# A fixed opening: squares summed on the vector engine as x lands, silu(c) behind the root, modulation dots two to a tile

## The chip, the cores and the metric

The kernel runs on one core of one Trainium2 chip. The metric is device microseconds of one execution. The core has a matrix engine (PE; its weight loads are listed apart as PEld), a vector engine (DVE), a scalar engine (ACT), GpSimd (POOL), and SyncE (SP), which issues most transfers. Each engine works through its own queue in the order in which the program was written or scheduled, and semaphores hold an instruction back until what it needs is there.

## The reference, cut to what matters

Two layers, each a half-step SwiGLU FFN, a mixing block and another half-step FFN. x is 512 tokens by 1024 channels. Only the entry to the first FFN is touched by the change:

```python
c_act = jax.nn.silu(c)
mod = (c_act @ w_ada[l] + b_ada[l]).reshape(B, N_MOD, D_MODEL)   # shift, scale, gate, three times
hn = rms_norm(h, g_ffn1[l]) * (1.0 + sc1) + sh1
h = h + 0.5 * (1.0 + gt1) * swiglu(hn, w_ffn1_in[l], w_ffn1_out[l])
# rms_norm: y = xf * lax.rsqrt(jnp.mean(xf * xf, axis=-1, keepdims=True) + EPS);  y * gain
```

## The kernel before, in words

x is kept transposed, as eight tiles `h[0]` to `h[7]` of 128 channels by 512 tokens; four transfers bring two tiles each. A float32 product is done as three products of rounded parts: high by high, high by low, low by high (`wH`, `wL` of a weight tile; `hnH`, `hnL` of the normed input). ACT makes each high part by a cast, DVE the low part by a subtraction.

**The opening (`begin`)** computes the first norm and the first six output tiles of the first FFN. Nearly every instruction is pinned behind the one before it on its engine, so the order is as written. Three parts:

1. The head. PE runs products without a use (`warm`, 128x512), then turns c into a row repeated over all partitions (`ps_crep`, 8 products); ACT takes silu of it into `crep`. The squares of the eight tiles are made on DVE and ACT, and PE sums them over channels by 32 products of one column (`summed`, L1374, four per tile, into `ps_ss`). ACT takes the root (L1390), DVE the reciprocal (L1391), and four PE products (L1394) spread it over the partitions in `ps_rstd`.
2. The list `PLAN`, a string of tokens worked through in order by `step`. `z<k>` is h[k] times `ps_rstd` on DVE; `ada<k>`, `part<k>`, `col<k>`, `gm<k>` get scale and shift of tile k (k = 0, 1, 2) from PE; `d<k>`, `e<k>` get them (k = 3 to 7) by two dots of 1024 elements against `crep` on DVE (L1404); `x<k>` applies them on ACT, `H<k>` and `L<k>` make the two parts; `wH<n>`, `wL<n>` split weight tile n; `W<n>` is n warm products. `P<n><k><p>` is one of 144 PE products: output tile n, input tile k, part p. Each runs through the line L1419 (L1408 after the change).
3. Transfers: `fetch` brings a pair of modulation columns (1 MB, `wada`, four buffers), `fetch_w` a weight tile (0.5 MB, `wfirst`, four buffers). `more` says behind which token the later ones are issued.

**PSUM buffers.** PSUM tiles are taken from tags with two buffers each. A tile takes the buffer of the tile two earlier on its tag, and its first writer waits for the last reader of that one. The six output tiles take the tags by `("r0", "r1", "mm")[n % 3]`. So tag r1 goes to `ps_rstd`, then output tile 1, then output tile 4, which gets the buffer of `ps_rstd`; the last reader of that is the last `z` token in the order.

**Behind the opening (`ffn`)**, ten more output tiles of the first FFN follow, each of 24 products (L127 to L129), with weights streamed through two `wraw` buffers; then products in pairs (`pair_in`, L431 to L433) begin. Between them, `ada_steps` puts dots of the next modulation vector (L197, 8 here, each against its own 0.5 MB transfer issued by POOL), spread over the tile pairs j by a tuple.

Of the kernel before, what the change touches and what calls it, by code (L numbers as in the profile page):

```python
# [17 lines left out]
P = 128  # L18
# [3 lines left out]
KD = D // P  # L22
# [4 lines left out]
NB = T // P  # L27
# [3 lines left out]
BASE = 16  # L31
PAD = 24
PLAN = """
z0 ada0 z1 z7 part0 wH0 W1 col0 z6 gm0 z2 W4 ada1 z4 x0 z3 H0 wL0 part1 P00a wH1 col1 L0 P00c P10a gm1 P00b P10b wL1 x1 ada2 H1 z5 P10c part2 P01a L1
P01c wH2 col2 P01b gm2 P11a wL2 P20a x2 P20b P11c P11b P21a H2 P21b d3 P20c P21c P02a wH3 P02c P12a P12c L2 P22a P22c P30a e3 P30b P31a P31b P02b P12b
P22b P32a wL3 P32b x3 H3 d4 W3 P30c P31c P32c P03a P03c P13a L3 P13c P23a P23c e4 wH4 P03b P13b P23b P33a P33c P33b P40a d5 P40b x4 P41a P41b P42a
P42b H4 P43a d6 P43b P04a P04c P14a wH5 P14c L4 P24a P24c P34a e6 P34c P50a P50b P51a P51b P52a P52b P53a wL5 x6 P53b P04b P14b P24b H6 P34b d7 P44a
P50c P51c P52c P53c P44b L6 P54a P54b P54c e5 P06a P06c P06b P16a P16c P16b P26a P26c e7 x5 P26b P36a P36c P36b H5 P46a P46b P56a wL4 x7 P05a P05c
P15a P15c H7 P25a L5 P25c P40c P41c P42c L7 P43c P44c P05b P15b P25b P35a P35c P35b P45a P45c P45b P55a P55c P55b P46c P56c P56b P07a P07c P07b P17a
P17c P17b P27a P27c P27b P37a P37c P37b P47a P47c P47b P57a P57c P57b  # L40
""".split()
GROUPS = ((0, 12), (12, 22))
STEP = 0.65
# [25 lines left out]
def trunk_kernel(ctx, tc, ins, out, layers=L, phases=("ffn1", "mix", "ffn2")):  # L69
# [12 lines left out]
    act, mm = nc.scalar.activation, nc.tensor.matmul  # L82

    def E(name="e", dt=F32):
        return sp.tile([P, T], dt, name=name, tag="e", bufs=4)
# [4 lines left out]
    def psum(shape, name, tag="x"):  # L90
        return ps.tile(shape, F32, name=name, tag=tag, bufs=2)
# [60 lines left out]
    h = []  # L152
# [84 lines left out]
    def new_ss():  # L237
        return sp.tile([P, T], F32, name="ss", tag="ss")
# [111 lines left out]
    def ffn(l, w_in, w_pair, w_out, hn, im, ss, need, then, first, ready, coming):  # L350
# [6 lines left out]
        with tc.tile_pool(name="act", bufs=1) as ap_:  # L357
# [153 lines left out]
            for g, (j0, j1) in enumerate(GROUPS):  # L511
                for p in range(j0 // 2, j1 // 2):
                    if p < n_first:
                        X = new_x(p)
                        for j in (2 * p, 2 * p + 1):
                            pg = next(tiles)
                            beside(2 * j)
                            pu = next(tiles)
                            s = E("silu")
                            act(pg.like(s), pg.view, AF.Silu)  # L520
                            for seen, part in pu.pieces(s):
                                stt(part, part, -1.0, seen, ALU.mult, ALU.mult)
                            nc.scalar.copy(xs[j][0], s)
                            behind = tt(xs[j][1], s, xs[j][0].bitcast(F32), ALU.subtract)
                            beside(2 * j + 1)
                            if n_first == 4:
                                ada_steps(ap_, crep, (4, 4, 0, 0, 0, 0, 0, 0)[j], behind)
                    else:
                        after[0] = None if g or p > n_first + 1 else loads[-2]
                        pair_in(p)  # L530
                        after[0] = None
                flush()
                if g and ss is not None:

                    act(E("none")[:, :1], xs[j1 - 1][0][:, :1].bitcast(F32), AF.Sqrt, bias=vals["eps"], scale=0.0)
                if todo and not crep:
                    with tc.issue_after(loads[-1].ins):
                        crep = ada_crep(ap_)
                if g == 0:
                    cg = small_.tile([P, KD], F32, name="cg", tag="cg")  # L540
                    if n_first == 4:
                        ada_until(ap_, crep, l, im + 2)
                k1 = 0
                for i in range(KD - 2 * g):
                    if i < 7 - g:
                        many = 3 * (i < 6) if not g else (2, 3, 3, 3, 3, 2)[i] if n_first == 4 else (3, 3, 3, 2, 2, 2)[i]
# [770 lines left out]
    def begin(pool):  # L1317
# [6 lines left out]
        def pin(e, m):  # L1324

            if e in behind:
                tc.add_manual_dep(m.ins, behind[e].ins.name, ORDER, reason="the opening keeps its order")
            behind[e] = m
            return m
# [3 lines left out]
        def fetch():  # L1333
            w = pool.tile([P, 2 * D], F32, name="wada", tag="wada", bufs=4)
            nc.sync.dma_start(w, ins["wa0"][len(wa)])
            wa.append(w)

        def fetch_w():
            j, g = divmod(len(wf), 2)
            w = pool.tile([P, KD, P], F32, name="wfirst", tag="wfirst", bufs=4)  # L1340
            nc.sync.dma_start(w, ins["w1i"][0, j, g])
            wf.append(w)

# [3 lines left out]
        def warm(n):  # L1347

            for _ in range(n):
                pin("PE", mm(pw.rearrange("p (a b) -> p a b", b=P), ones_r, wide, start=True, stop=True))  # L1350
# [3 lines left out]
        nc.gpsimd.tensor_copy(cz[:, :, 0], cact)  # L1354
        warm(3)
        crep = pool.tile([P, D], F32, name="crep", tag="crep")
        for hf in range(2):
            pt = psum([P, 4, P], "ps_crep")
            for k in range(4):
                pin("PE", mm(pt[:, k], cT[:, 4 * hf + k : 4 * hf + k + 1].to_broadcast([P, P]), cst("ident"), start=True, stop=True))  # L1360
            pin("ACT", act(crep[:, hf * 512 : hf * 512 + 512], pt.rearrange("p k n -> p (k n)"), AF.Silu))
            if hf == 0:
                sqs = [E("sq") for _ in range(2)]
                for i in range(2):
                    pin("ACT", act(sqs[i], h[i], AF.Square))
        pin("ACT", act(col["sh0"][:, :1], cact[:, :1], AF.Sqrt, bias=vals["eps"], scale=0.0))
        for _ in range(4):
            fetch()
            fetch_w()
        pt = psum([P, NB], "ps_ss")  # L1370

        def summed(i):
            for b in range(NB):
                m = mm(pt[:, b : b + 1], sqs[i][:, b * P : (b + 1) * P], ones[:, :1], start=i + b == 0, stop=i == KD - 1, skip_group_check=True)  # L1374
                pin("PE", m)

        summed(0)
        summed(1)
        for i in range(2, KD):
            sqs.append(E("sq"))  # L1380
            if i in (5, 7):
                pin("ACT", act(sqs[i], h[i], AF.Square))
            else:
                pin("DVE", tt(sqs[i], h[i], h[i], ALU.mult))
            if i % 2 == 0:
                warm(4)
            summed(i)
        warm(3)
        r = pool.tile([P, NB], F32, name="rstd_t", tag="rstd_t")
        pin("ACT", act(r, pt, AF.Sqrt, bias=vals["eps"], scale=1.0 / D))  # L1390
        pin("DVE", nc.vector.reciprocal(r, r))  # L1391
        rstd = psum([P, T], "ps_rstd", "r1")
        for b in range(NB):
            pin("PE", mm(rstd[:, b * P : (b + 1) * P], r[:, b : b + 1].to_broadcast([P, P]), cst("ident"), start=True, stop=True))  # L1394
        pin("DVE", stt(col["gb"], bsc, 1.0, g1, ALU.add, ALU.mult))
        zs, ws, part, sums, pts = {}, {}, {}, {}, {}

# [5 lines left out]
            w = wa[k][:, half : half + D]  # L1403
            pin("DVE", stt(w, w, 1.0, crep, ALU.mult, ALU.mult, accum_out=col[name][:, k : k + 1]))  # L1404

        more = {"ada0": (fetch,), "ada1": (fetch, fetch_w), "ada2": (fetch,), "wL1": (fetch_w,), "e3": (fetch,)}

        def step(token):  # L1408
            kind = "P" if token[0] == "P" else token.rstrip("0123456789")
# [10 lines left out]
                return  # L1420
            k = int(k)
            c = slice(k, k + 1)
            if kind == "z":
                zs[k] = pool.tile([P, T], F32, name="z", tag="z", bufs=KD)
                pin("DVE", tt(zs[k], h[k], rstd, ALU.mult))
# [156 lines left out]
```

## Time and profile before

| | |
|---|---|
| three runs | 1813.88, 1818.63, 1819.55 us; median 1818.63 us |
| the profiled execution | 1815.97 us, span 1814.2 us, granted clock 0.993 |
| busy share of the span | PE 98%, PEld 90%, DVE 74%, ACT 46%, POOL 8% |
| first P product | starts 31.08 us into the span |
| last P product of the opening | starts 65.68 us |
| first product of the pairs (L431) | starts 121.37 us |

A row of a timeline gives start, length, engine, line, operation, output and inputs, how many rows were merged, and in brackets how long the engine stood idle before it and what ended that. Matmul rows overlap each other, so successive starts, not lengths, give the pace of PE.

### The profile page before, as it was taken

The numbers are of one execution on the slowest core, as the hardware profiler recorded it, in microseconds if no ns is written. First come the engines' busy times: TensorE is split into PE (matmuls) and PEld (weight loads), VectorE is DVE, ScalarE is ACT, GpSimd is POOL, SyncE is SP. The second block draws the span as 40 slices with busy tenths as digits, with TensorE's granted clock in tenths as the row PEclk, the third lists the DMA queues.
The fourth block names the chain that finished last, engine by engine and source line by source line (L and its number), as shares of the span: only waits on it lengthen the run. The fifth ranks groups of instructions, "written<-read, shape, count | busy, mean of one in ns | idle before, by whom it ended". The sixth has DMA issues, their size and how long they took to land.

```text
span 1814.2 us, 33785 instructions
## 1 busy us (share of the span) xinstructions
PE 1785.9 (98%) x13898; PEld 1629.1 (90%) x13898; DVE 1347.8 (74%) x2181; ACT 840.0 (46%) x1292; POOL 142.8 (8%) x227
## 2 busy tenths in 40 slices
PE   9999999999999999999999999999999999999999
PEld 7789899898768999899999989999877798999998
DVE  4688677877777878678878786778686788864862
ACT  4444255374433555255445524544654445533551
POOL 0101100101000000100100010110000000010000
PEclk8999999999999999999999999999999999999999
DMA  8567877713123476976738687673421427685742
GB/s 313 190 194 208 271 198 204 249 53 102 57 83 119 140 201 177 303 192 192 239 107 214 177 284 205 187 230 130 122 64 41 141 79 196 186 235 137 200 140 70
DMA packets 91404, 309.93 MB, mean 171 GB/s; under 512 B 10416, under 2 KB 11184, under 8 KB 90224
## 3 DMA queue, kind: packets, MB, share of 16 engines
q1 hardware_dynamic: 61920, 201.58, 33.1%
q0 software_dynamic: 29328, 106.18, 23.5%
q8 instruction: 109, 1.79, 0.4%
q14 instruction: 47, 0.39, 0.1%
HBM read 303.79 MB, written 3.93 MB: 170 GB/s over the span
## 4 chain that ended last, share of the span: by engine, by line
PE 80%; DVE 9%; DMA 4%; ACT 4%; issue 2%; POOL 0%; ACTq 0%; DVEq 0%; SPq 0%; POOLq 0%
PE ps_mm L127 12%; PE ps_mm L128 12%; PE ps_mm L129 12%; PE ps_d L431 7%; PE ps_d L432 7%; PE ps_d L433 7%; PE ps_f L432 3%; PE ps_f L433 3%; PE ps_f L431 3%; DVE wL L141 2%; PE ps_g L432 2%; PE ps_g L433 2%; PE ps_g L431 2%; PE ps_mm L1419 2%; DMA wada<-in_wadaT 2%
## 5 line engine op out<-in xcount | busy, mean ns | idle before, releaser
L139 ACT CAST wH<-wraw 128x1024 fp32r<-128x1024 f32 (+2 forms) x290 | 264.0, 916 | 472.6 <-PE ps_mm L128 215.1
L141 DVE TENSOR_TENSOR wL<-wraw,wH 128x1024 fp32r<-128x1024 f32 (+2 forms) x290 | 306.0, 1059 | 120.1 <-ACT wH L139 118.3
L127 PE MATMUL ps_mm<-actH,wH 128*128 128x512 f32 (+1 forms) x784 | 281.0, 358 | 0.0
L128 PE MATMUL ps_mm<-actL,wH 128*128 128x512 f32 (+1 forms) x784 | 280.5, 358 | 0.0
L129 PE MATMUL ps_mm<-actH,wL 128*128 128x512 f32 (+1 forms) x784 | 280.5, 358 | 0.0
L129 PE MATMUL ps_mm<-hnH,wL 128*128 128x512 f32 (+1 forms) x712 | 245.0, 346 | 3.6 <-DVE wL L141 3.6
L127 PE MATMUL ps_mm<-hnH,wH 128*128 128x512 f32 (+1 forms) x712 | 247.3, 354 | 1.3 <-ACT hnH L289 0.9
L128 PE MATMUL ps_mm<-hnL,wH 128*128 128x512 f32 (+1 forms) x712 | 246.2, 348 | 0.1
L431 PE MATMUL ps_d<-comH,wH 128*128 128x256 f32 x816 | 225.2, 276 | 1.2 <-ACT s L457 1.2
L432 PE MATMUL ps_d<-comL,wH 128*128 128x256 f32 x816 | 224.4, 275 | 0.0
L433 PE MATMUL ps_d<-comH,wL 128*128 128x256 f32 x816 | 224.4, 275 | 0.0
L141 DVE TENSOR_TENSOR wL<-sum,wH 128x1024 fp32r<-128x1024 f32 x102 | 125.0, 1226 | 83.4 <-ACT wH L139 83.3
L197 DVE SCALAR_TENSOR_TENSOR wada<-wada,crep 128x1024 f32<-128x1024 f32 x128 | 153.5, 1221 | 37.5 <-DMA wada<-in_wadaT 37.3
L129 PEld LDWEIGHTS ps_mm<-actH,wL 128*128 128x128 f32 x784 | 148.7, 190 | 16.8
L128 PEld LDWEIGHTS ps_mm<-actL,wH 128*128 128x128 f32 x784 | 148.7, 190 | 16.7
L127 PEld LDWEIGHTS ps_mm<-actH,wH 128*128 128x128 f32 x784 | 148.7, 190 | 16.6
L431 PEld LDWEIGHTS ps_d<-comH,wH 128*128 128x128 f32 x816 | 156.6, 192 | 2.8 <-ACT s L457 2.8
L433 PEld LDWEIGHTS ps_d<-comH,wL 128*128 128x128 f32 x816 | 156.7, 192 | 0.0
L432 PEld LDWEIGHTS ps_d<-comL,wH 128*128 128x128 f32 x816 | 156.6, 192 | 0.0
L139 ACT CAST wH<-sum 128x1024 fp32r<-128x1024 f32 x102 | 106.8, 1047 | 105.0 <-PE ps_f L432 42.4
L127 PEld LDWEIGHTS ps_mm<-hnH,wH 128*128 128x128 f32 x712 | 133.5, 191 | 21.5 <-issue 7.6
L129 PEld LDWEIGHTS ps_mm<-hnH,wL 128*128 128x128 f32 x712 | 135.6, 190 | 17.8 <-DVE wL L141 4.8
(384 smaller groups left out, 3884.1 us busy)
## 6 DMA issues: line engine op xcount, KB each, us to landing
wada<-in_wadaT POOLq DMA_DIRECT2D x128, 512.0 KB, 4.8
wraw<-in_wmi SPq DMA_DIRECT2D x40, 512.0 KB, 3.6
wraw<-in_w2p SPq DMA_DIRECT2D x36, 512.0 KB, 4.2
wraw<-in_w1p SPq DMA_DIRECT2D x32, 512.0 KB, 5.0
wraw<-in_w1o SPq DMA_DIRECT2D x32, 384.0 KB, 4.5
wraw<-in_w2o SPq DMA_DIRECT2D x32, 384.0 KB, 4.5
wraw<-in_w1o SPq DMA_DIRECT2D x32, 320.0 KB, 4.0
wraw<-in_w2o SPq DMA_DIRECT2D x32, 320.0 KB, 3.5
```

What stands on the lines that cost most here:

```text
L127: mm(acc, wH, xH, start=start, stop=False)
L128: mm(acc, wH, xL, start=False, stop=False)
L129: latest["large"] = mm(acc, wL, xH, start=False, stop=stop)
L139: nc.scalar.copy(hi, src)
L141: return nc.vector.tensor_sub(lo, src, hi.bitcast(F32))
L197: stt(w, w, 1.0, crep, ALU.mult, ALU.mult, accum_out=out_)
L431: mm(acc, wH, xH, start=start and i + k == 0, stop=False, skip_group_check=True)
L432: mm(acc, wH, xL, start=False, stop=False, skip_group_check=True)
L433: mm(acc, wL, xH, start=False, stop=k == 3, skip_group_check=True)
L1419: latest["large"] = pin("PE", mm(paired(pts[n]), w, x, start=first, stop=last, skip_group_check=True))
```

## The change

Squares: ACT writes the square of h[0] straight into a sum tile `ss`, squares the others but h[3], and DVE adds them up as they come. The square of h[7] is not added: PE sums it and `ss` over channels by four one-column products each, 8 instead of 32. The root's activation table is loaded ahead of the squares, silu(c) moves behind the root (tokens `s0`, `s1`), the spreading of the reciprocal becomes a token (`R0`) behind `ada0`, fourteen warm products stand ahead of the 8 products, `wfirst` gets a fifth buffer, `PLAN` and `more` are new, and the eight dots in `ffn` are spread over four tile pairs.

```diff
-z0 ada0 z1 z7 part0 wH0 W1 col0 z6 gm0 z2 W4 ada1 z4 x0 z3 H0 wL0 part1 P00a wH1 col1 L0 P00c P10a gm1 P00b P10b wL1 x1 ada2 H1 z5 P10c part2 P01a L1
+ada0 R0 W1 s0 part0 wH0 col0 z0 gm0 s1 z4 W1 ada1 x0 z3 H0 z2 part1 P00a L0 wH1 col1 z1 P00b wH2 P10a wL1 P10b W1 P20a P20b gm1 P10c wL2 x1 ada2 H1
...
-                                ada_steps(ap_, crep, (4, 4, 0, 0, 0, 0, 0, 0)[j], behind)
+                                ada_steps(ap_, crep, (0, 2, 2, 2, 2, 0, 0, 0)[j], behind)
...
-            w = pool.tile([P, KD, P], F32, name="wfirst", tag="wfirst", bufs=4)
+            w = pool.tile([P, KD, P], F32, name="wfirst", tag="wfirst", bufs=5)
...
-        for hf in range(2):
-            pt = psum([P, 4, P], "ps_crep")
-            for k in range(4):
-                pin("PE", mm(pt[:, k], cT[:, 4 * hf + k : 4 * hf + k + 1].to_broadcast([P, P]), cst("ident"), start=True, stop=True))
-            pin("ACT", act(crep[:, hf * 512 : hf * 512 + 512], pt.rearrange("p k n -> p (k n)"), AF.Silu))
-            if hf == 0:
-                sqs = [E("sq") for _ in range(2)]
-                for i in range(2):
-                    pin("ACT", act(sqs[i], h[i], AF.Square))
         pin("ACT", act(col["sh0"][:, :1], cact[:, :1], AF.Sqrt, bias=vals["eps"], scale=0.0))
-        for _ in range(4):
-            fetch()
-            fetch_w()
+        turned = [psum([P, 4, P], "ps_crep", "r0") for _ in range(2)]
+        for k in range(KD):
+            pin("PE", mm(turned[k // 4][:, k % 4], cT[:, k : k + 1].to_broadcast([P, P]), cst("ident"), start=True, stop=True))
+        warm(14)
+        ss, sqs = new_ss(), {}
+        for i in range(KD):
+            if i:
+                sqs[i] = E("sq")
+            if i == 3:
+                pin("DVE", tt(sqs[3], h[3], h[3], ALU.mult))
+            else:
+                pin("ACT", act(sqs[i] if i else ss, h[i], AF.Square))
+            if i in (3, 4, 5, 6):
+                for j in range(1, 4) if i == 3 else (i,):
+                    pin("DVE", tt(ss, ss, sqs[j], ALU.add))
+        for f in (fetch, fetch_w, fetch, fetch_w, fetch_w, fetch, fetch_w, fetch):
+            f()
         pt = psum([P, NB], "ps_ss")
-        summed(0)
...
+        for n, x in enumerate((sqs[7], ss)):
             for b in range(NB):
+                pin("PE", mm(pt[:, b : b + 1], x[:, b * P : (b + 1) * P], ones[:, :1], start=n + b == 0, stop=n == 1, skip_group_check=True))
+        warm(2)
...
-        more = {"ada0": (fetch,), "ada1": (fetch, fetch_w), "ada2": (fetch,), "wL1": (fetch_w,), "e3": (fetch,)}
+        more = {"ada0": (fetch, fetch_w), "ada1": (fetch,), "wL0": (fetch_w, fetch), "e3": (fetch,)}
...
+            if kind == "R":
+                for b in range(NB):
+                    pin("PE", mm(rstd[:, b * P : (b + 1) * P], r[:, b : b + 1].to_broadcast([P, P]), cst("ident"), start=True, stop=True))
+            elif kind == "s":
+                pin("ACT", act(crep[:, k * 512 : k * 512 + 512], turned[k].rearrange("p k n -> p (k n)"), AF.Silu))
```

**Place 1: PE, the head.** `sq_149` to `sq_227` are the squares of h[0] to h[7], `wada_160` the first modulation columns. Before, from the second group of squares on:

```order
L1350 MATMUL ps_warm_135<-ones_r_100 128x512 x4
L1374 MATMUL ps_ss_176<-ones_r_100,sq_185 128x1 x4
L1374 MATMUL ps_ss_176<-ones_r_100,sq_195 128x1 x4
L1350 MATMUL ps_warm_135<-ones_r_100 128x512 x4
L1374 MATMUL ps_ss_176<-ones_r_100,sq_201 128x1 x4
L1374 MATMUL ps_ss_176<-ones_r_100,sq_211 128x1 x4
L1350 MATMUL ps_warm_135<-ones_r_100 128x512 x4
L1374 MATMUL ps_ss_176<-ones_r_100,sq_217 128x1 x4
L1374 MATMUL ps_ss_176<-ones_r_100,sq_227 128x1 x4
L1350 MATMUL ps_warm_135<-ones_r_100 128x512 x3
L1394 MATMUL ps_rstd_239<-con_83,rstd_t_236 128x128 x4
L1442 MATMUL ps_ada_247<-wada_160,cz_136 32x256 x8
```

After, `sq_188` is the square of h[7] and `ss_168` the sum of the other seven:

```order
L1360 MATMUL ps_crep_145<-con_83,cT_81 128x128 x4
L1350 MATMUL ps_warm_135<-ones_r_100 128x512 x14
L1378 MATMUL ps_ss_206<-ones_r_100,sq_188 128x1 x4
L1378 MATMUL ps_ss_206<-ones_r_100,ss_168 128x1 x4
L1350 MATMUL ps_warm_135<-ones_r_100 128x512 x2
L1436 MATMUL ps_ada_222<-wada_190,cz_136 32x256 x8
L1414 MATMUL ps_rstd_220<-con_83,rstd_t_217 128x128 x4
```

The one-column products are down to two groups of four, the warm products stand in one block, and the spreading has moved behind `ada0`.

**Place 2: PE, the first product of output tile 4 (`P40a`).** Before, as its row 91 (`ps_mm_420`), 48 P products come ahead of it:

```order
L1419 MATMUL ps_mm_376<-hnL_121,wH_367 128x512
L1419 MATMUL ps_mm_420<-hnH_114,wH_411 128x512 [waits Activation_49]
L1419 MATMUL ps_mm_420<-hnL_115,wH_411 128x512
L1419 MATMUL ps_mm_420<-hnH_116,wH_411 128x512
L1419 MATMUL ps_mm_420<-hnL_117,wH_411 128x512
```

After (`ps_mm_375`), 36 P products come ahead of it:

```order
L1408 MATMUL ps_mm_335<-hnH_118,wH_324 128x512
L1408 MATMUL ps_mm_335<-hnH_118,wL_325 128x512
L1408 MATMUL ps_mm_335<-hnL_119,wH_324 128x512
L1408 MATMUL ps_mm_375<-hnH_114,wH_367 128x512 [waits DVE_49,Activation_49]
L1408 MATMUL ps_mm_375<-hnL_115,wH_367 128x512
```

Output tile 4 comes 12 products earlier, and its first product now has a wait on DVE besides the one on ACT for its weights.

**Place 3: DVE, the last reader of `ps_rstd`.** Before, the last `z` (`z_335`, token `z5`) stands between the low parts of the second weight tile and of the second input tile:

```order
L1437 TENSOR_TENSOR wL_306<-wfirst_166,wH_305 128x1024 [waits DMAHW2_49,Activation_49]
L1425 TENSOR_TENSOR z_335<-h4_89,ps_rstd_239 128x512
L1431 TENSOR_TENSOR hnL_117<-z_258,hnH_116 128x512 [waits Activation_49]
L1399 SCALAR_TENSOR_TENSOR gm0_133<-ps_col_346,par_93,gb_130 128x1 [waits PE_49]
L1400 TENSOR_TENSOR sh0_134<-ps_col_346,par_93 128x1
```

After, it (`z_468`) stands behind all six weight splits, six low parts and eight of the ten dots; `wada_360` is the last modulation pair to be fetched:

```order
L1393 SCALAR_TENSOR_TENSOR wada_360,sc_131<-wada_360,crep_142 128x1024 [waits DMAHW4_49]
L1419 TENSOR_TENSOR z_449<-h6_91,ps_rstd_220 128x512
L1431 TENSOR_TENSOR hnL_127<-z_394,hnH_126 128x512 [waits Activation_49]
L1393 SCALAR_TENSOR_TENSOR wada_360,sh_132<-wada_360,crep_142 128x1024
L1388 SCALAR_TENSOR_TENSOR gm0_133<-sc_131,par_93,gb_130 128x1 [waits DVE_49]
L1389 TENSOR_TENSOR sh0_134<-sh_132,par_93 128x1 [waits DVE_49]
L1419 TENSOR_TENSOR z_468<-h4_89,ps_rstd_220 128x512
```

The `z` tokens were all early before; now `z6`, `z7` and `z5` come late, `z5` stands in PLAN behind 63 P tokens of which `P40a` is the first.

**Place 4: DVE, the dots behind the opening.** Before, `wL_649` is the split of the third weight tile there:

```order
L524 TENSOR_TENSOR actL_610<-silu_611,actH_609 128x512 [waits Activation_49]
L197 SCALAR_TENSOR_TENSOR wada_579,mod0_2_585<-wada_579,crep_562 128x1024 [waits DMASW2_49]
L197 SCALAR_TENSOR_TENSOR wada_581,mod0_2_585<-wada_581,crep_562 128x1024 [waits DMASW3_49]
L141 TENSOR_TENSOR wL_649<-wraw_647,wH_648 128x1024 [waits DMAHW0_49,Activation_49]
L197 SCALAR_TENSOR_TENSOR wada_583,mod0_2_585<-wada_583,crep_562 128x1024 [waits DMASW4_49,DVE_49]
```

After, that split is `wL_615`:

```order
L524 TENSOR_TENSOR actL_569<-silu_570,actH_568 128x512 [waits Activation_49]
L141 TENSOR_TENSOR wL_584<-wraw_582,wH_583 128x1024 [waits DMAHW7_49]
L141 TENSOR_TENSOR wL_615<-wraw_613,wH_614 128x1024 [waits DMAHW0_49,Activation_49]
L197 SCALAR_TENSOR_TENSOR wada_560,mod0_2_564<-wada_560,crep_540 128x1024 [waits DMAHW1_49,DMASW1_49]
L197 SCALAR_TENSOR_TENSOR wada_562,mod0_2_564<-wada_562,crep_540 128x1024 [waits DMASW2_49]
```

Three dots stood ahead of the third split; now none does.

More of the change, by code (lines that the diff above doesn't have):

```diff
@@ L33 @@
 PLAN = """
-z0 ada0 z1 z7 part0 wH0 W1 col0 z6 gm0 z2 W4 ada1 z4 x0 z3 H0 wL0 part1 P00a wH1 col1 L0 P00c P10a gm1 P00b P10b wL1 x1 ada2 H1 z5 P10c part2 P01a L1
[L35 to L40, printed above, removed]
+ada0 R0 W1 s0 part0 wH0 col0 z0 gm0 s1 z4 W1 ada1 x0 z3 H0 z2 part1 P00a L0 wH1 col1 z1 P00b wH2 P10a wL1 P10b W1 P20a P20b gm1 P10c wL2 x1 ada2 H1
+wL0 P20c part2 P01a P11a wH3 col2 L1 P00c P01c gm2 P30a P30b wL3 x2 P01b P11c P11b P21a H2 P21c d3 P21b P30c P31a P31b P31c P02a L2 P02c P12a P12c e3
+P22a P02b P12b P22c P22b wH4 P32a P32c P32b d4 x3 P40a P40b P41a P41b wL4 H3 P42a P42b P03a P03c P13a L3 P40c P41c wH5 P42c z6 P03b P13c P13b e4 P23a
+P23c P50a P50b P51a P51b P52a wL5 P52b x4 P23b P33a P33c P33b H4 P43a d6 P50c P51c P52c P43c P43b P53a L4 P53b P53c P04a e6 P04c P04b P14a P14c P14b
+P24a P24c d7 x6 P24b P34a P34c P34b H6 P44a P44c z7 P44b P54a P54c L6 P54b P06a P06c e7 P06b P16a P16c P16b P26a P26c P26b z5 P36a x7 P36c P36b P46a
+d5 P46c H7 P46b P56a P56c P56b L7 P07a P07c P17a e5 P17c P07b P17b P27a P27c P27b P37a P37c x5 P37b P47a P47c P47b H5 P57a P57c P57b L5 P05a P05c P15a
+P15c P05b P15b P25a P25c P25b P35a P35c P35b P45a P45c P45b P55a P55c P55b
 """.split()
@@ L1370, in begin @@
         pt = psum([P, NB], "ps_ss")
-        def summed(i):
+        for n, x in enumerate((sqs[7], ss)):
             for b in range(NB):
-                m = mm(pt[:, b : b + 1], sqs[i][:, b * P : (b + 1) * P], ones[:, :1], start=i + b == 0, stop=i == KD - 1, skip_group_check=True)
-                pin("PE", m)
-        summed(0)
[L1378 to L1387, printed above, removed]
@@ L1388, in begin @@
-        warm(3)
+                pin("PE", mm(pt[:, b : b + 1], x[:, b * P : (b + 1) * P], ones[:, :1], start=n + b == 0, stop=n == 1, skip_group_check=True))
+        warm(2)
         r = pool.tile([P, NB], F32, name="rstd_t", tag="rstd_t")
@@ L1392, in begin @@
         rstd = psum([P, T], "ps_rstd", "r1")
-        for b in range(NB):
-            pin("PE", mm(rstd[:, b * P : (b + 1) * P], r[:, b : b + 1].to_broadcast([P, P]), cst("ident"), start=True, stop=True))
         pin("DVE", stt(col["gb"], bsc, 1.0, g1, ALU.add, ALU.mult))
```

## The prediction

> **What bounds the kernel now.** First the page: PE is busy nearly throughout and its clock is full but for the first of 40 slices.
>
> ```profile
> PE 1785.9 (98%) x13898; PEld 1629.1 (90%) x13898; DVE 1347.8 (74%) x2181; ACT 840.0 (46%) x1292; POOL 142.8 (8%) x227
> PEclk8999999999999999999999999999999999999999
> ```
>
> So time can only be won where PE works on something else than products, or slowly: in the opening. Then the timeline of PE there, with where the products of the opening start and end and where the pairs begin, and below it windows (start and end, length, busy time of PE, PEld, DVE, ACT, POOL, granted clock, share of the DMA engines, GB/s).
>
> ```profile
> 2.38 1.65 PE L1350 MATMUL ps_warm<-ones_r 128*128 128x512 f32 x3 [2.38 <-ACT ones_r L165]
> 7.24 2.05 PE L1374 MATMUL ps_ss<-ones_r,sq 128*128 128x1 f32 x16
> 19.55 3.41 PE L1374 MATMUL ps_ss<-ones_r,sq 128*128 128x1 f32 x16
> 24.24 1.91 PE L1394 MATMUL ps_rstd<-con,rstd_t 128*128 128x128 f32 x8
> 30.08 1.07 PE L1442 MATMUL ps_ada<-wada,cz 128*32 128x256 f32 x16
> 31.08 0.48 PE L1419 MATMUL ps_mm<-hnH,wH 128*128 128x512 f32 x1
> 65.68 0.38 PE L1419 MATMUL ps_mm<-hnL,wH 128*128 128x512 f32 x1
> 65.89 0.46 PE L127 MATMUL ps_mm<-hnH,wH 128*128 128x512 f32 x1
> 121.37 0.27 PE L431 MATMUL ps_f<-comH,wH 128*128 128x256 f32 x1
> ```
>
> ```profile
> 7.66:11.07 3.41, 3.41 (x27) 3.24 (x28) 1.55 (x3) 2.52 (x4) 0.00 (x0) 1.00 1.04 427
> 11.07:14.48 3.41, 3.41 (x14) 3.02 (x14) 0.69 (x1) 0.63 (x1) 0.00 (x0) 0.50 1.03 423
> 24.72:28.13 3.41, 3.41 (x24) 1.92 (x23) 1.94 (x4) 0.05 (x1) 0.00 (x0) 0.50 0.02 8
> 28.13:31.00 2.87, 2.87 (x25) 1.61 (x25) 2.39 (x6) 2.71 (x4) 0.00 (x0) 1.00 0.52 174
> ```
>
> PE is never without a row in the head, yet from 7.24 to 26 these are one-column products, warm products and the spreading, which lead to the root and no further; from 11.07 to 28.13 they run at half clock (the same sixteen rows take 3.41 in place of 2.05). Transfers fill that time at over 400 GB/s and then stop (8 GB/s), since no buffer is free. From 31.08 PE runs products at 65.89 - 65.68 = 0.21 us each (0.2155 by longer stretches of such rows).
>
> **The change: the head.** Eight groups of one-column products become two, while squares and adds hide under the landing of x.
>
> ```profile
> 1.65 1.85 SPq L155 DMA_DIRECT2D h<-in_xT  x4
> DMA to landing us min/median/max: 4.3/5.5/6.7
> 7.22 2.08 DVE L1384 TENSOR_TENSOR sq<-h 128x512 f32<-128x512 f32 x3 [6.19 <-DMA h<-in_xT]
> 8.10 1.28 ACT L1366 ACT_TABLE_LOAD   x1
> 22.99 0.26 ACT L1390 ACTIVATE rstd_t<-ps_ss,v_eps 128x4 f32<-128x4 f32 x1 [9.61 <-PE ps_ss L1374]
> 23.29 0.18 DVE L1391 RECIPROCAL rstd_t<-rstd_t 128x4 f32<-128x4 f32 x1 [11.46 <-ACT rstd_t L1390]
> 26.19 2.48 DVE L1425 TENSOR_TENSOR z<-h,ps_rstd 128x512 f32<-128x512 f32 x4 [2.67 <-PE ps_rstd L1394]
> 28.35 1.05 ACT L1435 CAST wH<-wfirst 128x1024 fp32r<-128x1024 f32 x1
> 29.47 0.82 ACT L1427 ACTIVATE z<-z,sh,gm 128x512 f32<-128x512 f32 x1
> 30.32 0.62 ACT L1429 CAST hnH<-z 128x512 fp32r<-128x512 f32 x1
> ```
>
> The last pair of x lands at 3.1 + 6.7 = 9.8. Two squares on ACT end near 11.0, the sixth add on DVE (7.22 + 7 x 0.69) near 12.1; the fourteen warm products, of 512 columns like the P products (0.2155 each), fill PE from 7.4 to 10.5, when the square they stand ahead of is not ready either, so they cost nothing; at the pace of the first three (1.65 / 3 = 0.55) they would run to 15 and cost 4. Four products on the sum take 2.05 / 4 = 0.5 to 1.0: the sum stands by 13.1, root and reciprocal (22.99 to 23.47) add 0.5. On PE two warm products and `ada0` (0.5 + 1.07) come first: 14.7; the spreading takes 0.96 to 1.91. So z0 starts at 15.8, at half clock 17.3, against 26.19. Silu(c), moved behind the root, brings a table load and two activations in front of `x0` on ACT: from the root at 13.5 the load 1.28, the two silus and the copy for `part0` at some 0.6 each (as the cast of 512 columns at 30.32), the cast of the first weight tile 1.05, x0 0.82 and H0 0.6 add up to 5.6 and end at 19. Its cover is z0, `gm0` and three more z on DVE until 18.7; what shows of the move is about 0.5, and 1 to 2 if the load comes late. The first P product comes near 19 in place of 31.08.
>
> On SP the first eight loads keep their bytes; the third weight tile goes ahead of the third modulation pair, and the fifth `wfirst` buffer lets the fifth weight tile go out without waiting for a split. POOL's one store of `crep` stays behind DVE's last work of the opening. I cost these at nothing by themselves: what counts is when the last modulation pair lands, below.
>
> **The change: output tile 4.** That gain meets a wait. `ps_rstd`, output tile 1 and output tile 4 share the two buffers of tag r1, so `P40a` waits for the last reader of `ps_rstd`, `z5`. Before, it is read early:
>
> ```profile
> 34.21 0.68 DVE L1425 TENSOR_TENSOR z<-h,ps_rstd 128x512 f32<-128x512 f32 x1
> ```
>
> At 34.2 nothing waits for it; now `z5` is the 42nd instruction of DVE from z0 on, behind dots that wait for transfers. PE gets 36 of the 144 products done and stops; the 108 others are queued behind it, though ACT has the parts of more input tiles ready, and everything of the FFN waits for PE. When z5 is read comes out of DVE's sum, by successive starts:
>
> ```profile
> 44.40 0.22 DVE L1399 SCALAR_TENSOR_TENSOR gm<-sc,par,gb 128x1 f32<-128x1 f32 x1
> 44.60 1.22 DVE L1404 SCALAR_TENSOR_TENSOR wada<-wada,crep 128x1024 f32<-128x1024 f32 x1
> 45.75 1.22 DVE L1404 SCALAR_TENSOR_TENSOR wada<-wada,crep 128x1024 f32<-128x1024 f32 x1
> 46.89 0.69 DVE L1431 TENSOR_TENSOR hnL<-z,hnH 128x512 fp32r<-128x512 f32 x1
> 48.84 1.22 DVE L1437 TENSOR_TENSOR wL<-wfirst,wH 128x1024 fp32r<-128x1024 f32 x1
> 49.98 1.22 DVE L1404 SCALAR_TENSOR_TENSOR wada<-wada,crep 128x1024 f32<-128x1024 f32 x1
> ```
>
> Eight dots and six weight splits at 1.14, eight z and six low parts at 0.61, seven pairs of gm and sh at 0.20: 16.0 + 8.5 + 1.4 = 25.9. From 15.8 to 17.3 that gives 41.7 to 43.2 with no wait in it. Transfers bound it too:
>
> ```profile
> wada<-in_wa SPq DMA_DIRECT2D x8, 1024.0 KB, 7.5
> wfirst<-in_w1i SPq DMA_DIRECT2D x6, 512.0 KB, 10.4
> 21.31:24.72 3.41, 3.41 (x14) 3.12 (x15) 0.23 (x2) 0.26 (x1) 0.00 (x0) 0.50 0.79 321
> ```
>
> The first loads, up to the fourth pair and the fourth weight tile, end near 24 as now (321 GB/s in the last row, 423 when full); four more of 1.05 MB and two of 0.52 MB at 423 GB/s end at 36.5, or 38.5 if some 2 us are lost between them; d7, z7, L6, e7, gm and z5 behind the last add 4.3: 41 to 43. With some waits for weights on both, I take z5 read at 44.0 (42.4 to 46).
>
> PE has its 36 done near 29 to 30: the last part that they need, L2, is DVE's 11.2 us of work after z0 (15.8 + 11.2 = 27, and a little for waits), with eight products behind it. So the stop is some 14 us long. PE's longest wait in the trace of before, once it has begun, is 2.3:
>
> ```profile
> PE ps_t L659 <- DVE X L996: 4.6, 2, 2.3
> ```
>
> So what 14 us do to the clock isn't seen, and is bounded: nothing (a gain is excluded, full clock being the most that the rows show), or half clock as in the 17.1 us from 11.07 to 28.13 (a loss of 8.5). Nearest is the start of the program: PE runs from 2.38, and the products are at their fast pace only from about 7.4, 5 us at half pace, a loss of 2.5. I take 2.5.
>
> [...]
>
> Then 108 products: 44.1 + 108 x 0.2155 + 2.5 = 69.9 for the first L127, against 65.89: 4.0 later. Bounds: 42.5 + 23.3 = 65.8 with no loss of clock (0.1 earlier) and 46.1 + 23.3 + 2.5 = 71.9 (6.0 later); the 8.5 is rival B.
>
> **The change: dots behind the opening.** From 65.89 to 121.37 PE does 240 products, 51.7 us, so 3.8 are lost:
>
> ```profile
> PE ps_mm L129 <- DVE wL L141: 3.1, 2, 1.8
> 76.30 1.23 DVE L197 SCALAR_TENSOR_TENSOR wada<-wada,crep 128x1024 f32<-128x1024 f32 x1 [0.65 <-DMA wada<-in_wadaT]
> 77.45 1.22 DVE L141 TENSOR_TENSOR wL<-wraw,wH 128x1024 fp32r<-128x1024 f32 x1
> 95.28 1.23 DVE L141 TENSOR_TENSOR wL<-wraw,wH 128x1024 fp32r<-128x1024 f32 x1 [2.16 <-ACT wH L139]
> ```
>
> DVE waits in a dot for POOL's transfer, the weight split queued behind comes late, and PE waits for it. Now the third split stands ahead of the dots, ready near L127 + 6 where it is needed at + 10.5, and later splits have 4 us or more in hand: both stalls go. Two dots (2.4 us) move to where DVE idled (95.28); DVE and ACT reach the pairs with less lead over PE, so I charge 0.4 to the waits there: 3.8 - 0.4 = 3.4 gained (1.8 if only the first stall goes, 3.8 at most). The table load that falls away there (ACT finds silu's table loaded) lay where PE had products: nothing.
>
> **Sum.** +4.0 - 3.4 = +0.6, bounds -0.1 - 3.8 = -3.9 and 6.0 - 1.8 = +4.2. Behind that the queues are the same. The profiled execution, 1815.97 (span 1814.2 and 1.8 around it), becomes 1816.6; it lies 2.7 under the median 1818.63, which becomes **1819.2**. About 0.3%, 5.5 us, is what a measurement of this kernel can tell from no change.
>
> **Rivals.** *A, the wait does not bind* (`P40a` waits only for the z written ahead of it). With the first product at 19 and 34.8 us to L127 as now (65.89 - 31.08), L127 comes at 53.8, 12.1 earlier, with 3.4 more behind it, against the median: 1803. For it: no such wait shows in the trace of before. Against: the two-buffer tag and the reader that stands last. Chance 0.07.
>
> *B, slower: the clock stays low after the stop.* In the trace it stayed at half for 17.1 us although PE's rows were gapless; that again costs 8.5 in place of 2.5: 1825.2. It decides from a stretch of (5.5 - 0.6 + 2.5) x 2 = 15 us. Against: those rows were one-column products, here they are dense. Chance 0.13. [...]
>
> *C, the later stalls stay*, since PE's next wait there is a transfer and not the order: +4.0 alone, 1822.6, and over the bound with z5 at 46: chance 0.17, a third of it over.
>
> *D, z5 early and no clock lost*: 1814.7. Chance 0.1.
>
> **How the numbers follow.** The forecast itself has the remaining 0.53. Faster by over 0.3%: A and a little of D, 0.10. Slower: B, and a third of C, 0.19. Within: 0.71. The range reaches from D less the spread of runs (1813.88 to 1819.55) to B: 1812 to 1826.
>
> **What would show it.** Right: 8 one-column products, z0 near 16 to 17, a PE gap of 12 to 16 us before the first product of output tile 4, ended by DVE's last z at about 44; half clock behind it for some 5 us; first L127 near 70; no wait for `wL` behind the opening; first L431 near 122. Wrong: no such gap (A), a clock row of 0.50 past 58 (B), or wL waits that stay (C).

## The result, and the profile after

| | before | after |
|---|---|---|
| median, range of 12 runs each | 1818.10 us, 1813.88 to 1824.84 | 1816.93 us, 1815.21 to 1821.22 |
| ratio after to before | | 0.9994, 95% interval 0.9982 to 1.0006 |
| profiled execution, span | 1815.97, 1814.2 us | 1821.22, 1819.2 us |

No change that can be measured: 1.2 us less by the medians, between 3.3 less and 1.1 more by the interval; the prediction had 0.6 more (1819.2, in a range of 1812 to 1826). The spans differ by 5.0 because the profiled execution of after is the longest of its twelve. So the traces are compared by landmarks, not by their ends.

The page of after, busy time of PE and its clock:

```profile
PE 1778.3 (98%) x13846; PEld 1620.3 (89%) x13846; DVE 1349.7 (74%) x2186; ACT 841.2 (46%) x1295; POOL 142.5 (8%) x227
PEclk8999999999999999999999999999999999999999
```

PE is busy 7.6 us less and nothing is gained by it: what was taken out of its head stands again as idle time. The timeline of PE in after shows where, with the first and the last `z` of DVE (`z0`, `z5`) and its six adds in the last three rows:

```profile
11.28 1.05 PE L1378 MATMUL ps_ss<-ones_r,sq 128*128 128x1 f32 x8 [0.68 <-ACT sq L1369]
12.71 1.05 PE L1378 MATMUL ps_ss<-ones_r,ss 128*128 128x1 f32 x8 [0.37 <-DVE ss L1372]
16.21 1.76 PE L1414 MATMUL ps_rstd<-con,rstd_t 128*128 128x128 f32 x8
20.45 0.48 PE L1408 MATMUL ps_mm<-hnH,wH 128*128 128x512 f32 x1 [0.56 <-ACT hnH L1423]
31.15 0.38 PE L1408 MATMUL ps_mm<-hnL,wH 128*128 128x512 f32 x1
44.00 0.77 PE L1408 MATMUL ps_mm<-hnH,wH 128*128 128x512 f32 x1 [12.47 <-DVE z L1419]
69.47 0.38 PE L127 MATMUL ps_mm<-hnH,wH 128*128 128x512 f32 x1
121.27 0.27 PE L431 MATMUL ps_f<-comH,wH 128*128 128x256 f32 x1
8.04 4.61 DVE L1372 TENSOR_TENSOR ss<-ss,sq 128x512 f32<-128x512 f32 x6
18.02 0.69 DVE L1419 TENSOR_TENSOR z<-h,ps_rstd 128x512 f32<-128x512 f32 x1 [3.69 <-PE ps_rstd L1414]
43.17 0.68 DVE L1419 TENSOR_TENSOR z<-h,ps_rstd 128x512 f32<-128x512 f32 x1
```

The first product of the opening comes 10.6 us earlier than before (20.45 against 31.08). Then PE stands idle for 12.47 us at the first product of output tile 4, and what ended the wait is a `z` on DVE. The first L127 is 3.6 us later than before, the first L431 0.1 us earlier: the opening's loss is made good by the ten output tiles behind it.

The chain of work that ended last, in after (start, length, what), names the step from `z5` to `P40a`, and DVE as the engine ahead of it:

```profile
41.91 1.15 DVE wada L1393 x2
43.26 0.61 DVE z L1419
43.87 0.14 issue
44.00 22.84 PE ps_mm L1408 x95
```

Windows of after (columns as in the prediction: PE's busy time third, the granted clock third from the end) in the head, around the stop, and at the first pairs:

```profile
10.68:14.09 3.41, 2.44 (x18) 2.16 (x18) 1.76 (x3) 0.82 (x4) 0.00 (x0) 1.00 1.02 418
14.09:17.50 3.41, 3.41 (x24) 1.89 (x23) 0.23 (x2) 3.02 (x4) 0.00 (x0) 0.50 1.00 405
31.16:34.57 3.41, 0.37 (x2) 0.00 (x0) 3.41 (x6) 1.92 (x3) 0.00 (x0) 1.00 1.03 424
34.57:48.22 13.65, 4.22 (x10) 3.44 (x11) 12.38 (x28) 5.50 (x8) 0.00 (x0) 0.50 0.45 181
48.22:51.63 3.41, 3.41 (x17) 2.98 (x17) 0.69 (x1) 0.23 (x1) 0.70 (x1) 1.00 0.26 107
126.74:130.15 3.41, 1.80 (x14) 1.42 (x13) 3.41 (x4) 3.01 (x5) 0.00 (x0) 1.00 1.00 225
130.15:133.56 3.41, 3.41 (x19) 3.41 (x18) 1.80 (x2) 0.57 (x1) 0.00 (x0) 0.50 0.71 246
```

The clock is at half from 34.57 to 48.22, for the last part of the stop and the first 4.2 us of work behind it, and in two places more up to the pairs (14.09 and 130.15). PE's waits from 60 to 130, in after:

```profile
PE ps_g L433 <- DVE wL L141: 0.9, 1, 0.9
PE ps_d L431 <- ACT s L457: 0.7, 1, 0.7
```

The two waits for `wL` ahead of the pairs (3.1 us) are gone. At the pairs there are 1.6 us of waits against 1.0 before, and behind them 3.41 us at half clock from 130.15, in which PE is busy throughout: they cost 1.7, half their length, and the trace of before does not have them. By the first product on L659 for `ps_c`, the next landmark, after is 2.2 us behind (the row gives shortest, median and longest in ns, then first and last start), before and then after:

```profile
L659 PE MATMUL ps_c<-AR,a x256: 218/218/268, 419.1 to 1346.4; 64*64 64x64 f32 x128
```

```profile
L659 PE MATMUL ps_c<-AR,a x256: 217/218/268, 421.3 to 1351.1; 64*64 64x64 f32 x128
```

The terms are -0.1 + 0.6 + 1.7 = 2.2. The 2.8 us by which the two spans part behind that are not explained here. The engines have as many instructions there as before, and both traces have two more stretches of 3.4 us at half clock (from 506.00 and 1478.80 before, from 509.03 and 1396.49 after), so neither more work nor more half-clock stretches are the reason.

### The profile page after: what moved, and what is told of

Same layout as the page of the kernel before. It is cut to its first block, busy times and chain, and to the rows that moved or that the text cites. A ratio compares the mean times of both kernels' runs of the same rounds, so it can differ in the third digit from the quotient of the medians.

```text
span 1819.2 us, 33688 instructions
## 1 busy us (share of the span) xinstructions
PE 1778.3 (98%) x13846; PEld 1620.3 (89%) x13846; DVE 1349.7 (74%) x2186; ACT 841.2 (46%) x1295; POOL 142.5 (8%) x227
## 4 chain that ended last, share of the span: by engine, by line
PE 76%; DVE 12%; DMA 6%; ACT 3%; issue 3%; POOL 0%; SPq 0%; ACTq 0%; DVEq 0%; POOLq 0%
PE ps_mm L127 11%; PE ps_mm L128 11%; PE ps_mm L129 11%; PE ps_d L431 7%; PE ps_d L432 7%; PE ps_d L433 7%; PE ps_f L432 3%; PE ps_f L433 3%; PE ps_f L431 3%; DVE wL L141 2%; DMA wada<-in_wadaT 2%; DVE wada L197 2%; PE ps_g L432 2%; PE ps_g L433 2%; PE ps_g L431 2%
## 5 line engine op out<-in xcount | busy, mean ns | idle before, releaser
L127 PE MATMUL ps_mm<-actH,wH 128*128 128x512 f32 (+1 forms) x784 | 281.4, 359 | 0.6 <-ACT wH L139 0.6
L127 PE MATMUL ps_mm<-hnH,wH 128*128 128x512 f32 (+1 forms) x712 | 247.1, 353 | 1.7 <-ACT hnH L289 1.3
L431 PE MATMUL ps_d<-comH,wH 128*128 128x256 f32 x816 | 226.4, 277 | 0.8 <-ACT s L457 0.7
L127 PEld LDWEIGHTS ps_mm<-actH,wH 128*128 128x128 f32 x784 | 148.9, 190 | 17.4 <-ACT wH L139 1.0
L431 PEld LDWEIGHTS ps_d<-comH,wH 128*128 128x128 f32 x816 | 157.5, 193 | 2.3 <-ACT s L457 2.3
L127 PEld LDWEIGHTS ps_mm<-hnH,wH 128*128 128x128 f32 x712 | 133.4, 190 | 21.9 <-issue 8.0
L129 PEld LDWEIGHTS ps_mm<-hnH,wL 128*128 128x128 f32 x712 | 135.6, 190 | 13.8 <-DVE wL L141 1.0
```

The lines of the kernel that those rows point to most:

```text
L127: mm(acc, wH, xH, start=start, stop=False)
L129: latest["large"] = mm(acc, wL, xH, start=False, stop=stop)
L431: mm(acc, wH, xH, start=start and i + k == 0, stop=False, skip_group_check=True)
```

## Experiments: the stop

**The three late `z` moved ahead (e1).** In PLAN `z6`, `z7` and `z5` leave their places and stand behind `L2`:

```diff
-... P02a L2 P02c ... wH5 P42c z6 P03b ... P44c z7 P44b ... P26b z5 P36a
+... P02a L2 z6 z7 z5 P02c ... wH5 P42c P03b ... P44c P44b ... P26b P36a
```

> The three multiplications z6, z7 and z5 are moved ahead, behind L2, so that the last reader of ps_rstd comes near 31 us instead of 43.9; all other orders stay. Theory of the prediction (the stop of PE is output tile 4 waiting for the buffer that ps_rstd holds): the wait of 12.5 us is gone, P40a starts near 31, the 108 products behind it take 23.3 us and some waits for parts, first L127 between 54.8 and 57 in place of 69.47, no half-clock stretch behind 31; time 12 to 14.5 us under the changed kernel, near 1803. Rival 1 (the stop is really DVE's or the transfers' pace, and the buffer only its last wait): other waits take its place, first L127 at 60 or later, gain under 9 us. Rival 2 (the gain of the opening is lost in the gated weights behind it, which wait for transfers): L127 near 56, but first L431 later than 112, where the present 51.8 us between them would give about 107.

**The order kept, the buffer released (e2).** ACT copies `ps_rstd` to SBUF, and the late `z` read the copy:

```diff
-x0 z3 H0 z2 part1
+x0 z3 H0 c0 z2 part1
-                pin("DVE", tt(zs[k], h[k], rstd, ALU.mult))
+                pin("DVE", tt(zs[k], h[k], part["rs"] if k > 4 else rstd, ALU.mult))
+            elif kind == "c":
+                part["rs"] = pool.tile([P, T], F32, name="rs", tag="rs")
+                pin("ACT", nc.scalar.copy(part["rs"], rstd))
```

> The order of the changed kernel is kept; ACT copies ps_rstd into SBUF behind H0 (some 0.6 us) and z6, z7 and z5 read the copy, so that the last reader of the PSUM buffer is z1 near 22 us. Theory (it is the buffer, not the place of z6, z7 and z5 in DVE's order): the same as with the early z: no wait of P40a, first L127 between 55 and 58, time near 1804. Rival (the place of the z in the order matters by itself, for their input parts come late): P40a starts near 31, but later products wait, first L127 at 60 or later.

e1: 1805.58 us, ratio to before 0.9916 (0.9895 to 0.9938). e2: 1801.54 us, 0.9898 (0.9873 to 0.9922). The last reader of `ps_rstd` in e1 (the three `z` in one row) and its first L127; then e2's last `z`, as late as in after but reading `rs`, and its first L127:

```profile
29.82 1.87 DVE L1419 TENSOR_TENSOR z<-h,ps_rstd 128x512 f32<-128x512 f32 x3
56.85 0.38 PE L127 MATMUL ps_mm<-hnH,wH 128*128 128x512 f32 x1
```

```profile
43.39 0.70 DVE L1419 TENSOR_TENSOR z<-h,rs 128x512 f32<-128x512 f32 x1
54.89 0.38 PE L127 MATMUL ps_mm<-hnH,wH 128*128 128x512 f32 x1
```

The wait of 12.5 us is in neither. e2 changes nothing in DVE's order, and its last `z` is as late as after's (43.39 against 43.17); only the PSUM buffer is free earlier. So it is the buffer that held PE up, and neither DVE's pace nor the transfers': with it free, the first L127 comes 14.6 us earlier than in after. The gain is kept behind the opening too (first L431 at 106.69, 51.80 behind the first L127, as in after). e1's first L127 is within its expectation, 2 us behind e2's, with 1.6 us of waits for parts.

**The stop filled (e4).** 55 warm products ahead of `P40a`:

```diff
-wH4 P32a P32c P32b d4 x3 P40a P40b
+wH4 P32a P32c P32b d4 x3 W55 P40a P40b
```

> The changed kernel with 55 more warm products ahead of P40a, which fill 11.9 of the 12.5 us in which PE waits and add no result. Theory (the half clock from 35 to 48.4 comes from PE standing idle, and costs 2.2 us of the products): clock 1.00 all along, P40a again at 44.0, 108 products in 23.3 us, first L127 at 67.3 instead of 69.5; time 2.2 us lower, near 1815. Rival (the low clock behind the stop has another cause, or comes back when the products begin): L127 stays at 69.5. If the warm products run on at half clock they end late, and P40a comes after 44.

1815.07 us, ratio 0.9976 (0.9961 to 0.9991). In the trace, the warm products, the last `z`, `P40a` and the first L127; and a window behind `P40a`:

```profile
33.19 12.63 PE L1350 MATMUL ps_warm<-ones_r 128*128 128x512 f32 x55
44.94 0.68 DVE L1419 TENSOR_TENSOR z<-h,ps_rstd 128x512 f32<-128x512 f32 x1
45.76 0.45 PE L1408 MATMUL ps_mm<-hnH,wH 128*128 128x512 f32 x1
69.15 0.38 PE L127 MATMUL ps_mm<-hnH,wH 128*128 128x512 f32 x1
```

```profile
45.76:48.22 2.46, 2.46 (x13) 2.17 (x13) 2.46 (x4) 0.73 (x2) 0.00 (x0) 1.00 0.03 7
```

The 67.3 that was expected is missed, since this execution's `z5` was 1.8 us later than after's (its first product, at 22.07, was already 1.6 later) and the warm products, begun late, ran until `P40a`. But from `P40a` to the first L127 it is now 23.39 us, against 25.47 in after and 108 x 0.2155 = 23.27 without a loss. So the clock costs the changed kernel 2.2 us, and it is PE's idleness that loses it here: from 34.57 to 48.22 the clock is at 0.50 in after, and at 1.00 in e4, with the gap filled. By the ratios e4 is 3.3 us under after, with intervals that overlap.

## Experiments: the dots behind the opening

**The old dots in the changed kernel (e3), the new dots in the kernel before (e5), the old dots in the kernel with the copy (e9).** Each is one line, in e5 the other way round:

```diff
-ada_steps(ap_, crep, (0, 2, 2, 2, 2, 0, 0, 0)[j], behind)
+ada_steps(ap_, crep, (4, 4, 0, 0, 0, 0, 0, 0)[j], behind)
```

> The changed kernel with the dots behind the opening in their old places (4, 4, 0, ...). Theory of the prediction (the order of the dots made the two waits for wL): both waits come back, some 3.1 us, and from the first L127 to the first L431 it is near 55 us instead of 51.8; time 3 us above the changed kernel, near 1820. Rival (the stalls went because L127 comes 3.6 us later and the transfers through POOL do not, so that they are further along): no or one short wait, 51.8 to 53 us between the two, time within 1.5 us of the changed kernel.

> The kernel before with nothing changed but the places of the dots behind the opening: (0, 2, 2, 2, 2, 0, 0, 0) in place of (4, 4, 0, ...). With the old dots in the changed kernel the two long waits for wL stayed away (0.3 us of them before the first L431), so the prediction's 3.4 us would belong to the place of the third weight split, which the opening's new order brings ahead of the dots, and not to the new places of the dots. Theory 1 (the place of the split): here the third split still stands behind three dots, so the waits for wL between 65.9 and 121.4 stay, 2 to 3.1 us, and the time is that of before within 1.5 us. Theory 2 (the places of the dots): the waits go, first L431 near 118, time 3 us lower.

> The kernel with the copy of ps_rstd (first L127 at 54.89, first L431 at 106.7, 1801.5 us) with the dots behind the opening in their old places. In DVE's order the third weight split stays ahead of the dots here, as in the changed kernel. Theory 1 (the place of the third split ends the waits, the places of the dots are worth little): first L431 at 107 to 107.5, waits for weights at the pairs of 1.5 to 3 us in place of 1.6, time within 2 us of the kernel with the copy, between 1801 and 1804. Theory 2 (the places of the dots are worth the 3.4 us, and in the earlier run with them L127 only came too late to show it): first L431 near 110, time near 1805.

| | ratio to before | first L127 | first L431 | first `ps_c` |
|---|---|---|---|---|
| before, old dots | 1 | 65.89 | 121.37 | 419.1 |
| e5: before, new dots | 1.0006 (0.9992 to 1.0021) | 65.89 | 119.76 | 418.5 |
| after, new dots | 0.9994 (0.9982 to 1.0006) | 69.47 | 121.27 | 421.3 |
| e3: after, old dots | 1.0003 (0.9986 to 1.0019) | 70.16 | 122.49 | 425.2 |
| e2: copy, new dots | 0.9898 (0.9873 to 0.9922) | 54.89 | 106.69 | 405.1 |
| e9: copy, old dots | 0.9945 (0.9931 to 0.9959) | 54.88 | 106.68 | 410.8 |

First the split of the third weight tile on DVE: in e3 it runs in one row with the second (x2), ahead of the dots, and the row starts 3.3 us behind the first L127; in e5 it stands behind three dots, 11.5 us behind the first L127, as in before.

```profile
73.46 2.35 DVE L141 TENSOR_TENSOR wL<-wraw,wH 128x1024 fp32r<-128x1024 f32 x2
```

```profile
77.38 1.22 DVE L141 TENSOR_TENSOR wL<-wraw,wH 128x1024 fp32r<-128x1024 f32 x1
```

PE's waits from 60 to 135, of e5, then of e9:

```profile
PE ps_mm L129 <- DVE wL L141: 1.7, 1, 1.7
PE ps_g L433 <- DVE wL L141: 0.9, 1, 0.9
PE ps_d L431 <- ACT s L457: 0.7, 1, 0.7
```

```profile
PE ps_g L433 <- DVE wL L141: 1.6, 1, 1.6
PE ps_d L433 <- DVE wL L141: 0.8, 1, 0.8
PE ps_g L431 <- ACT wH L139: 0.5, 1, 0.5
PE ps_d L431 <- ACT s L457: 0.2, 1, 0.2
```

Neither simple theory holds. That the two waits for `wL` ahead of the pairs go is mostly the place of the third split, and that comes with the opening's new order: e3 has the old dots and loses 52.33 - 51.80 = 0.5 us there, and in e5 one of the two waits stays at 1.7. It is not that the first L127 comes later, the rival of e3: in e9 it comes 11.0 us earlier than before, again with the old dots, and the first L431 follows 51.80 behind. But the places of the dots matter one stage later: with the old ones DVE and ACT come late to the pairs. e9 has 3.1 us of waits there where e2 has 1.6, and it loses the clock, which e2 does not:

```profile
115.60:122.43 6.83, 6.35 (x28) 6.06 (x29) 4.31 (x5) 2.69 (x4) 0.00 (x0) 0.50 0.74 236
```

1.5 of waits and 3.2 for 6.35 us of work at half clock are 4.7 of the 5.7 us by which e9 is behind at `ps_c`; its ratio is 0.0035, or 6.4 us, above that of e10 below, and its median of 1808.25 us lies above what either theory expected. In the changed kernel the old dots cost nothing that the ratios show, though the trace of e3 is 3.9 us behind that of after at `ps_c`; in the kernel before the new ones bring nothing. What the places of the dots are worth by themselves, then, depends on what stands around them.

## Experiments: the head, and the version to keep

**Spreading first (e6), warm products in the gaps (e7), both, with the later copy (e8), a later copy alone (e10)**, all on top of e2:

```diff
# e6
-ada0 R0 W1 s0 part0 wH0 col0 z0 gm0 s1 z4 W1 ada1 x0 z3 H0 c0 z2 part1
+R0 ada0 s0 part0 wH0 W1 col0 z0 gm0 z4 W1 ada1 x0 z3 H0 c0 z2 s1 part1
# e7
-        warm(14)
+        warm(17)
...
+            if n:
+                warm(3)
# e10
-H0 c0 z2 part1 ... x1 ada2 H1
+H0 z2 part1 ... x1 ada2 H1 c0
```

> The kernel with the copy of ps_rstd, and the spreading of the root ahead of ada0 instead of behind it, the second silu behind H0. If PE's products from 20.3 on are gapless and set the end of the opening, the chain to the first of them is what counts: z0 comes 1 to 1.5 us earlier, the first product near 19.0, first L127 near 53.5 in place of 54.89, time 1.4 us under the kernel with the copy. Rival (the first modulation column or the first weight tile ends the wait, not z0): the first product stays at 20.3, no difference.

> The kernel with the copy of ps_rstd, 17 warm products in place of 14 ahead of the one-column products and three more between their two groups, where PE stood idle for some 0.4 to 0.7 us. Half clock then lasted from about 14.8 to 21.2 in the kernel with the copy (between 3.4 and 10 us in the other runs). Theory (it is the idle stretches beside the one-column products that lose the clock): clock 1.00 from 11 to 22, spreading and ada0 in 1.0 to 1.1 us each, first product near 19, time 1 to 2 us lower. [...]

> Both edits of the head together (spreading first, warm products in the gaps), and the copy of ps_rstd behind H1 instead of H0, where it doesn't hold up z1. If both work: first product near 18, first L127 between 52.3 and 53.5, time 2 to 3 us under the kernel with the copy, near 1799. If DVE's order of low parts and splits sets the pace from the first product on, PE waits for parts instead, and first L127 stays above 54.

> The kernel with the copy of ps_rstd with the copy moved from behind H0 to behind H1 on ACT, some 3 to 4 us later, so that z1 does not wait 0.83 us for it and the first parts of ACT come 0.6 us earlier; P40a, near 31, still finds the buffer free. If the early products are held up by DVE's and ACT's parts: first L127 at 54 to 54.5 in place of 54.89, time 0.5 us lower; if PE's own row of work from 20.3 on sets it: no difference. In either case near 1801, at least 14 us under the changed kernel, by which this is the version to keep.

| | median | ratio to before | first product | first L127 |
|---|---|---|---|---|
| e2 | 1801.54 us | 0.9898 (0.9873 to 0.9922) | 20.30 | 54.89 |
| e6 | 1803.00 us | 0.9912 (0.9892 to 0.9931) | 18.77 | 55.46 |
| e7 | 1802.72 us | 0.9910 (0.9893 to 0.9927) | 18.43 | 54.31 |
| e8 | 1802.88 us | 0.9913 (0.9898 to 0.9927) | 19.89 | 54.85 |
| e10 | 1801.32 us | 0.9910 (0.9896 to 0.9923) | 21.50 | 56.12 |

In e6 and e7 the first product comes 1.5 to 1.9 us earlier, and in e7 and e8 the clock stays at 1.00 through the head, where e2 is at half from 14.6 to 21.4. A window of e7, one of e2, and two of e6:

```profile
11.00:14.50 3.50, 3.50 (x34) 2.53 (x33) 0.97 (x4) 1.33 (x2) 0.00 (x0) 1.00 1.04 426
```

```profile
14.80:21.20 6.40, 6.40 (x33) 4.32 (x33) 3.15 (x7) 4.98 (x9) 0.00 (x0) 0.50 1.02 413
```

```profile
8.55:11.97 3.42, 3.42 (x20) 2.92 (x18) 3.07 (x5) 1.79 (x4) 0.00 (x0) 1.00 1.03 420
11.97:15.38 3.41, 3.40 (x31) 2.58 (x34) 0.78 (x3) 2.14 (x3) 0.00 (x0) 1.00 1.02 419
```

So eight rows of one-column products do not lose the clock by themselves. That the gaps beside them do is not shown. e6 has none of the added products and keeps the clock too, up to 22.2; in its trace PE has no gap there either (busy for 6.82 of the 6.83 us of the last two rows). But in before PE had none from 7.66 to 11.07, and there the clock fell at 11.07. Part of e6's earlier first product can be the clock's: `ada0` takes 1.07 us in it, and 1.94 at half clock in after. In any case a full clock in the head is worth nothing here: the first L127 does not follow, and the times are the same. An earlier first product finds the parts of the next tiles not ready; e7 has waits of 0.8, 0.4, 0.4 and 0.3 us there for ACT and DVE, so these set the pace, and not PE alone. The expectations of 1 to 3 us less were wrong. e10's later copy shows no difference in the times either; in its trace the first L127 comes 1.2 us later than in e2, and not 0.5 earlier. The version to keep is e2 or e10, by the medians 15 to 17 us under before and after.

## Why the prediction was right, point by point

- **The head.** Sum at 13.8 instead of 13.1: the six adds ended at 12.65, by 0.77 each and not 0.69. Then 3.41 us at half clock (14.09 to 17.50) fell on `ada0` and the spreading, which took 1.94 and 1.76 us, some 0.8 more each than the prediction's 1.07 and 0.96, and z0 started at 18.02, 2.2 behind 15.8 and 0.7 behind the upper bound of 17.3. That bound had 1.5 for the half clock, about what it took, though the working names only the spreading; for a late sum it had nothing. The term that was mis-sized is the adds. The first product came at 20.45, not near 19.
- **The stop.** `z5` was read from 43.17 to 43.85 and `P40a` began at 44.00, against 44.0 and 44.1. From z0 that is 25.8 us, and the sum had 25.9; the margin that I added for waits was not needed, and the late z0 used it up; that the two nearly cancel is luck. DVE has no gap between z0 and z5 (busy for all of the 25.15 us from 18.02 to 43.17), so its own work set the time, and not the transfers. PE had its 36 products done at 31.5 and not near 29 to 30, so the stop was 12.5 us and not 14, which changes nothing behind it. That the buffer and nothing else made the stop is shown by e2: rival A had the mechanism's absence at 1803, and with the buffer free it is 1801.5.
- **The clock.** Charged 2.5, measured 2.2 (e4). Rival B's stretch of 15 us of work at half clock did not come: 4.2 us behind `P40a`. The fall came 3.0 us behind the end of the last product (34.57 against 31.53), the rise 4.2 us behind `P40a` (48.22 against 44.00). The 2.5 was the author's estimate from the start of the program; that a stop loses as much as that start is not shown, only the 2.2 at this stop.
- **First L127** at 69.47, against 69.9.
- **The dots.** Term -3.4; to the first L431 it was -3.7 (55.48 us before, 51.80 after). The mechanism, the third split ahead of the dots, was right, but I put it under the change of the dots, and e3, e5 and e9 show that it comes mostly with the new opening. The 0.4 charged at the pairs was 0.6 of waits, and 1.7 for the clock, which no term held.
- **The sum** was +0.6. The trace has -0.1 at the first L431 and +2.2 at the first `ps_c`; the runs say -1.2 (-3.3 to +1.1). It was near by a cancelling of two large terms that were each sized well, and of small ones that were not; that these cancelled too is luck.

## What to carry to other kernels

When instructions are reordered, look for every buffer whose last reader moves: here a rotating buffer turned a late read into a stop of 12.5 us of the engine that was to write next, and a copy, put at some 0.6 us before its run, was worth 15.4 by the medians (e2 against after). A stage that is made to start earlier can lose it at its next wait (10.6 us won at the first product, 3.6 lost by the first L127), so follow the new order to the end of the stage, engine by engine. The stop cost its length and the clock behind it (2.2 us), and that second part was seen by filling the stop with work that has no use (e4).

## What the runs showed of the hardware that was not expected

**The same short waits went with a lost clock in one run and with a full clock in another.** After and e2 have the same two waits at the first pairs (0.9 and 0.7 us). In after PE was busy for 1.80 of the 3.41 us in which both fell, and the next 3.41 us were at half clock (the last two rows of the windows of after, in the section on the result). In e2 PE was busy for 1.79 of the 3.40 us in which both fell, and the clock stays:

```profile
112.30:115.70 3.40, 1.79 (x14) 1.47 (x13) 3.40 (x4) 3.01 (x5) 0.00 (x0) 1.00 0.95 205
115.50:122.30 6.80, 6.80 (x63) 6.80 (x62) 4.87 (x6) 3.85 (x5) 0.04 (x1) 1.00 0.62 214
```

In e1, too, two waits of 1.1 and 0.7 us fell into 3.41 us, PE was busy for 1.79, and the clock stayed:

```profile
114.57:117.98 3.41, 1.79 (x13) 1.60 (x14) 3.41 (x4) 3.02 (x5) 0.00 (x0) 1.00 0.93 195
117.98:121.39 3.41, 3.41 (x33) 3.41 (x32) 1.53 (x2) 1.82 (x3) 0.00 (x0) 1.00 0.75 248
```

In e9 and e3 PE was busy for 1.61 and 1.65 us of the 3.4 us ahead of a half-clock stretch (112.20 to 115.60, and 124.17 to 127.58). So these busy times do not part the runs that lost the clock from those that kept it, and what does is not shown; no run moved the waits alone.

**Before and after show half clock in multiples of one length.** In after it lasted 3.41 us from 14.09 and from 130.15, and 13.65, four times as long, from 34.57; in before 17.06, five times as long, from 11.07. After's three starts lie 20.48 and 95.58 us apart, 6.0 and 28.0 times the 3.41. What sets this is not shown.

**PE lost the clock without a gap.** In before PE was busy for all of the 3.41 us from 7.66 to 11.07, with one-column and warm products, and the clock was at half from 11.07 to 28.13 all the same. In e7 and e8 warm products stood between the two groups of one-column products, and the clock stayed at 1.00 (from 11.00 to 22.00 in both).
